# Attention of a two-layer trunk on one core: the order of its transposes, value products and scores on TensorE, and the layout of 768 keys

## The chip, the cores and the metric

The kernel runs on 1 core of one Trainium2 chip. The metric is the device time of one execution in microseconds; shown is the median of several executions. Where a profile is read, it is the profile of one execution.

## The reference, cut to what matters

A latent stream x of 512 tokens (a grid 64 wide) and 256 context tokens y pass two layers of width 1024. In each layer one input projection of 2976 columns feeds four mixers with 4 heads each; their 4 x 256 outputs go through one output projection into a gated residual, then a SwiGLU block of hidden width 2816 follows. Three of the mixers are softmax attention, and they are what the change touches:

```python
def softmax_attend(q, k, v, scale, sink=None):
    s = einsum('bhqd,bhkd->bhqk', q, k) * scale        # sink: one more logit
    return einsum('bhqk,bhkd->bhqd', softmax(s), v)
# mla: latent queries read 512 latent + 256 context keys, q and k of 64 + 32 rotary columns
# na:  neighbourhood attention, 8 x 16 of the grid, with a bias, and the 256 context keys, one softmax
# swa: windowed attention, 128 keys to either side, the context keys and a sink logit
# context queries read the 256 context keys only, in all three (layer 0; in layer 1 only x goes on)
```

The fourth mixer is a bidirectional chunkwise retention. Everything is float32.

## The kernel before, in words

Tokens are handled in tiles of 128: tiles 0 to 3 are latent, 4 and 5 context (in layer 1 only 0 to 3 as queries). A dense product is made of three matmuls (`mm3`, L467 to L469): weights and activations are split into a high part and a remainder.

**Weights.** A block of weights, 512 KB as a rule, is loaded into a tile `raw` (four buffers in the kernel before: the line `CHANGED`), copied by ScalarE into `wh` (L449), and the remainder `wl` is made by VectorE or, one time in three, by GpSimd (`sub_lo`, L213). After these two the raw buffer is free. `load_nat` does this for a projection: 8 row blocks of 128, two to a block, so 4 blocks for 512 columns; its loads are on SyncE's queue (L459). The feed-forward weights are loaded from ScalarE's queue (L1454, L1494).

**Stages of a layer.** `na_proj` (two projections), `na_attn`, `swa_proj`, `swa_attn`, `ret_proj` (two projections), `mla_proj` with the retention chunks `ret_chunk`, then a loop over the tiles `mo`: MLA attention of a tile (`mla_attn`), a number of half output projections that don't need it (`rest`, numbers `FILL`), `merge_mla`, which splits the result for the output projection, and `finish`, the other half, with the norm for the feed-forward block. Then the feed-forward block in 11 groups of 256 hidden columns.

**Attention of a tile.** `q_stack` loads q, transposes it (L669), and splits it into `qa` by ScalarE (L673) and `qb` by VectorE (L674); MLA adds a rotary part (L989 to L993). For each head: scores into PSUM tiles `s` (`scores`, L633; L935 to L937 in na, L1142 to L1147 in swa), the minimum of the negated scores (MLA: L1007, two pieces of 384 keys, and L1009), the exponential on ScalarE with its sum (L1012, L1155, L1157, L946), and the division `norm_p` (L614, L620). `attend_T` then transposes the probabilities P (L586) into PSUM tiles `t` and copies them to `PT`, the first four blocks by ScalarE (L589), the rest by VectorE (L591). `attend_pv` makes the value products of two heads (a pair) into a tile `o` (L599).

**What sets the order.** The program is traced in the order of the code, and a planner then orders each engine's instructions: it runs the program on a model of its own, takes what is ready, and so moves instructions of later stages ahead of ones that wait. Each kind of tile has a fixed number of buffers (`s` 4 of the PSUM banks, `t` 2, `o` 2, `P` 6, `PT` 4, `qT` 3, `wh` 5, `wl` 7, `raw` 4); the planner places them in memory and makes an instruction wait for a buffer. On the chip an engine runs its queue in that order.

Of the kernel before, what the change touches and what calls it, by code (L numbers as in the profile page):

```python
# [16 lines left out]
P = 128  # L17
# [60 lines left out]
CHANGED = {'pad': {'raw': 1024}, 'bufs': {'raw': 4}}  # L78
# [9 lines left out]
def build(tc, I, out, opts=None):  # L88
# [85 lines left out]
    TR = (opts or {}).get("tr", ("ldq", "ldq", "xn"))  # L174
    PRI = {}
# [459 lines left out]
    def soft_y(q_of, k_of, v_of, negsink=None, sk=None):  # L635

        pv = PS("o")
        sums = S("s2", 8).rearrange("p (h a) -> p h a", h=H)
        m = S("m4", 4)
        for hp in range(2):  # L640
            A = PS("s")
            for e in range(2):
                h = 2 * hp + e
                scores(A[:, 256 * e:256 * e + 256], q_of(h), k_of(h))
# [4 lines left out]
            PTs = []  # L649
            for e in range(2):  # L650
# [7 lines left out]
                PTs.append(attend_T(Pm, 2))  # L658
            attend_pv(pv, hp, PTs, [v_of(2 * hp), v_of(2 * hp + 1)])
        return pv  # L660
# [150 lines left out]
    for l in range(LAYERS):  # L811
# [28 lines left out]
        def na_proj():  # L840
# [76 lines left out]
            def na_attn():  # L917
                st = T("st", [P, 2, NT])
                for t in () if last else ytiles:
                    o = soft_y(q_stack(qn_d[rows(t), :], -0.125), lambda h: [kTn[h][:, NX:NT]] * 2,  # L920
                               lambda h: [Vyn[:, i, h * 64:(h + 1) * 64] for i in range(2)])
                    put(o, st[:, :, rows(t)])
                for cb in range(4):
# [3 lines left out]
                    qs_ = q_stack(qn_d[rows(cb), :], -0.125)  # L927
                    pv = PS("o")
                    sums = S("s4", 4)
                    for h in range(H):  # L930
# [3 lines left out]
                        q2 = qs_(h)  # L934
# [11 lines left out]
                        act.activation(Pm, A, AF.Exp, bias=m[:, 0:1], scale=-1.0, accum_out=sums[:, h:h + 1])  # L946
                        dsl = slice(h * 64, (h + 1) * 64)
                        if h % 2 == 0:
                            PTs, vs = [], []
                        vs.append([Vw[(2 * cb + b) // 3][:, (2 * cb + b) % 3, dsl] for b in range(2)]  # L950
                                  + [Vyn[:, b, dsl] for b in range(2)])
                        norm_p(Pm, sums[:, h:h + 1])
                        PTs.append(attend_T(Pm, 4))
                        if h % 2:
                            attend_pv(pv, h // 2, PTs, vs)
                    put(pv, st[:, :, 0:NX].rearrange("p a (r c) -> p a r c", c=64)[:, :, :, 16 * cb:16 * cb + 16])
# [4 lines left out]
        def mla_proj(R):  # L961
# [19 lines left out]
            def mla_attn(t):  # L981
# [12 lines left out]
                qof = lambda h: q2(h) + [qr[:, h, :]]  # L994
                kof = lambda h, a, b: [kTm[h][:, a:b], kTm[h][:, a:b], kTr[:, a:b]]
                vof = lambda h, js: [Vm[j // 3][:, j % 3, h * 64:(h + 1) * 64] for j in js]
                if t >= 4:
                    return soft_y(qof, lambda h: kof(h, NX, NT), lambda h: vof(h, (4, 5)))
                pv = PS("o")
                s2 = S("s2", 8).rearrange("p (h a) -> p h a", h=H)  # L1000
                for h in range(H):
                    m2 = S("m2", 2)
                    A = []
                    for i in range(2):
                        A.append(PS("s")[:, 0:384])
                        scores(A[i], qof(h), kof(h, 384 * i, 384 * i + 384))
                        dve.tensor_reduce(m2[:, i:i + 1], A[i], axis=AX.X, op=ALU.min)  # L1007
                    m = S("m1", 1)
                    dve.tensor_tensor(m, m2[:, 0:1], m2[:, 1:2], op=ALU.min)  # L1009
                    Pm = T("P", [P, 768])  # L1010
                    for i in range(2):
                        act.activation(Pm[:, 384 * i:384 * i + 384], A[i], AF.Exp, bias=m[:, 0:1], scale=-1.0,  # L1012
                                       accum_out=s2[:, h, i:i + 1])
                    if h % 2 == 0:
                        PTs = []
                    norm_p(Pm, s2[:, h])
                    PTs.append(attend_T(Pm, 6))
                    if h % 2:
                        attend_pv(pv, h // 2, PTs, [vof(h - 1, range(6)), vof(h, range(6))])
                return pv  # L1020
# [26 lines left out]
            for t, ps in nat_block(w_in, 0, 416, hT, order, (lambda t: (0, 416) if (t < 4 or not last) else (160, 416))):  # L1047
# [52 lines left out]
                yield mla_attn  # L1100

        def swa_proj():
# [18 lines left out]
            def swa_attn():  # L1121
                st = T("st", [P, 2, NT])
                for t in (0, 1, 2, 3) + (() if last else ytiles):
                    qof = q_stack(q_d[rows(t), 384:640], -0.125)
                    vof = lambda h, js: [Vs[:, j, 64 * (h // 2):64 * (h // 2) + 64] for j in js]
                    if t >= 4:
                        o = soft_y(qof, lambda h: [kTs[h // 2][:, NX:NT]] * 2, lambda h: vof(h, (4, 5)),
                                   negsink=sinkn[:, l], sk=sink[:, l])
                    else:
                        lo_b = max(t - 1, 0)  # L1130
                        hi_b = min(t + 1, 3)
                        blks = list(range(lo_b, hi_b + 1))
                        nl = len(blks)
                        pv = PS("o")
# [403 lines left out]
```

## Time and profile before

| | us |
|---|---|
| median of 3 runs | 1907.11 |
| lowest and highest | 1906.93, 1912.47 |
| the profiled execution | 1910.68 |
| its span (first to last instruction) | 1908.8 |

The profiled execution is longer than its span by what lies around it. In all rows times are microseconds unless marked ns; PE is TensorE's matmul, PEld its weight load, DVE VectorE, ACT ScalarE, POOL GpSimd, SP SyncE, and a q behind a name is that engine's DMA queue. L and a number is a line of the kernel. Busy time counts pipelined matmuls with modelled ends, so a busy PE is not PE at its peak. `[0.96 <-DMA raw]` at the end of a row is the idle time of that engine just before, and what ended it.

### The profile page before, as it was taken

The numbers are of one execution on the slowest core, as the hardware profiler recorded it, in microseconds if no ns is written. First come the engines' busy times: TensorE is split into PE (matmuls) and PEld (weight loads), VectorE is DVE, ScalarE is ACT, GpSimd is POOL, SyncE is SP. The second block draws the span as 40 slices with busy tenths as digits, with TensorE's granted clock in tenths as the row PEclk, the third lists the DMA queues.
The fourth block names the chain that finished last, engine by engine and source line by source line (L and its number), as shares of the span: only waits on it lengthen the run. The fifth ranks groups of instructions, "written<-read, shape, count | busy, mean of one in ns | idle before, by whom it ended". The sixth has DMA issues, their size and how long they took to land. (4 is left out here: it accounts for less than half of the span.)

```text
span 1908.8 us, 28192 instructions
## 1 busy us (share of the span) xinstructions
PE 1811.7 (95%) x10447; PEld 1494.0 (78%) x10447; DVE 1187.5 (62%) x2676; ACT 672.9 (35%) x1517; POOL 605.2 (32%) x560
## 2 busy tenths in 40 slices
PE   6899999889999999999999999899889999999997
PEld 3677777778889887888888878788777888888885
DVE  5696886877898757564434293465588863434335
ACT  3325643254542221221122233564255532222223
POOL 0211113323115443444344111211333144645542
PEclk9999999899999999999999999999999999999999
DMA  7675436445124346342222222422443033232321
GB/s 226 210 206 162 131 98 187 127 151 117 50 95 127 122 155 199 105 134 63 74 67 67 57 84 91 120 75 81 143 142 100 15 115 101 84 107 89 102 86 44
DMA packets 193555, 215.22 MB, mean 113 GB/s; under 512 B 66660, under 2 KB 141578, under 8 KB 193418
## 3 DMA queue, kind: packets, MB, share of 16 engines
q10 hardware_dynamic: 75840, 111.17, 18.8%
q1 hardware_dynamic: 117578, 102.25, 18.1%
q8 instruction: 82, 1.34, 0.3%
q14 instruction: 55, 0.45, 0.1%
HBM read 192.76 MB, written 20.63 MB: 112 GB/s over the span
## 5 line engine op out<-in xcount | busy, mean ns | idle before, releaser
L469 PE MATMUL pg<-wh,b 128*128 128x512 f32 (+2 forms) x1128 | 439.9, 394 | 7.2 <-POOL b L213 6.2
L467 PE MATMUL pg<-wh,b 128*128 128x512 f32 (+2 forms) x1128 | 443.1, 393 | 1.8 <-ACT b L515 0.9
L468 PE MATMUL pg<-wl,b 128*128 128x512 f32 (+2 forms) x1128 | 441.5, 391 | 2.2 <-DVE rs_yn L288 1.8
L467 PE MATMUL ps<-b,wh 128*128 128x512 f32 (+1 forms) x1120 | 388.2, 347 | 0.0
L469 PE MATMUL ps<-b,wl 128*128 128x512 f32 (+1 forms) x1120 | 386.7, 345 | 0.8 <-DVE wl L213 0.8
L468 PE MATMUL ps<-b,wh 128*128 128x512 f32 (+1 forms) x1120 | 386.9, 345 | 0.5 <-POOL b L213 0.5
L213 DVE TENSOR_TENSOR wl<-raw,wh 128x1024 fp32r<-128x1024 f32 (+1 forms) x131 | 207.4, 1592 | 174.9 <-ACT wh L449 145.3
L449 ACT ACTIVATE wh<-raw 128x1024 fp32r<-128x1024 f32 (+1 forms) x196 | 203.8, 1049 | 271.1 <-PE pg L469 172.3
L213 POOL TENSOR_TENSOR wl<-raw,wh 128x1024 fp32r<-128x1024 f32 (+1 forms) x65 | 160.0, 2462 | 336.7 <-ACT wh L449 286.8
L1362 POOL TENSOR_TENSOR b<-b,nat 128x512 f32<-128x512 f32 (+1 forms) x204 | 217.8, 1087 | 124.0 <-DVE nat L1360 95.0
L469 PEld LDWEIGHTS pg<-wh,b 128*128 128x128 f32 x1128 | 214.9, 191 | 49.6 <-POOL b L213 9.6
L467 PEld LDWEIGHTS pg<-wh,b 128*128 128x128 f32 x1128 | 215.5, 191 | 40.9 <-ACT b L1476 1.9
L468 PEld LDWEIGHTS pg<-wl,b 128*128 128x128 f32 x1128 | 215.2, 191 | 39.7 <-DVE rs_yn L288 2.3
L467 PEld LDWEIGHTS ps<-b,wh 128*128 128x128 f32 x1120 | 213.5, 191 | 27.4 <-issue 2.4
L469 PEld LDWEIGHTS ps<-b,wl 128*128 128x128 f32 x1120 | 213.4, 191 | 26.0 <-DVE wl L213 1.0
L468 PEld LDWEIGHTS ps<-b,wh 128*128 128x128 f32 x1120 | 213.6, 191 | 25.5 <-POOL b L213 0.7
L1360 DVE TENSOR_TENSOR nat<-pg,gate 128x512 f32<-128x512 f32 x240 | 161.9, 688 | 102.0 <-PE pg L469 97.8
L1473 ACT ACTIVATE P<-ps 128x512 f32<-128x512 f32 (+1 forms) x70 | 35.4, 505 | 224.3 <-PE ps L469 128.0
L1475 DVE TENSOR_TENSOR P<-ps,P 128x512 f32<-128x512 f32 (+1 forms) x70 | 40.1, 575 | 118.9 <-PE ps L469 118.8
L1476 ACT ACTIVATE b<-P 128x512 fp32r<-128x512 f32 (+1 forms) x70 | 37.6, 538 | 195.3 <-DVE P L1475 176.0
L397 DVE SCALAR_TENSOR_TENSOR PT<-qT,consts,PT 128x512 f32<-128x512 f32 x112 | 94.0, 857 | 14.6 <-DMA qT<-in_ada_w_dram 13.3
L213 POOL TENSOR_TENSOR b<-P,b 128x512 fp32r<-128x512 f32 (+1 forms) x24 | 27.8, 1158 | 231.9 <-ACT b L1476 231.9
(322 smaller groups left out, 2441.7 us busy)
## 6 DMA issues: line engine op xcount, KB each, us to landing
raw<-in_ffn_w_dram ACTq DMA_DIRECT2D x132, 512.0 KB
qT<-in_ada_w_dram ACTq DMA_DIRECT2D x96, 256.0 KB
raw<-in_w_in_dram SPq DMA_DIRECT2D x40, 512.0 KB
a<-in_ada_w_dram SPq DMA_DIRECT2D x32, 256.0 KB
a<-in_ada_w_dram ACTq DMA_DIRECT2D x32, 256.0 KB
xn<-in_ada_w_dram ACTq DMA_DIRECT2D x32, 256.0 KB
raw<-in_w_out_dram SPq DMA_DIRECT2D x16, 512.0 KB
ldq<-q_d SPq DMA_DIRECT2D x40, 128.0 KB
```

The lines of the kernel that those rows point to most:

```text
L213: eng.tensor_tensor(out, full, hi.bitcast(F32), op=ALU.subtract)
L397: dve.scalar_tensor_tensor(acc[s], w, sS[:, k, s:s + 1], acc[s], op0=ALU.mult, op1=ALU.add)
L449: act.activation(hi, raw_ap, AF.Copy)
L467: pe.matmul(ps, a[0], b[0], start=first, stop=False)
L468: pe.matmul(ps, a[0], b[1], start=False, stop=False)
L469: pe.matmul(ps, a[1], b[0], start=False, stop=last)
L1360: dve.tensor_tensor(tm, ps, gates[(0 if t < 4 else 2) + b], op=ALU.mult)
L1362: eng.tensor_tensor(ap, ap, tm[:, a:c], op=ALU.add)
L1473: act.activation(s1[j][:, sl], ps, AF.Silu)
L1475: dve.tensor_tensor(s1[j][:, sl], ps, s1[j][:, sl], op=ALU.mult)
L1476: act.activation(gh[j][:, sl], s1[j][:, sl], AF.Copy)
```

## The change

The attention functions no longer run a head after the other. Each returns or pushes jobs, one for a pair of heads (`hp`), with a function `s` that traces the scores and the softmax and gives the two P tiles, and a function `fin` for what is to be done with the result. `Flow` takes the jobs with a depth of 2: when a third pair is pushed, a turn is traced first, which has the transposes of the oldest pair's second head, the value products of the pair before it, and the transposes of its first head; then come the scores of the pushed pair. `part` uses `tc.issue_after`: each TensorE instruction traced inside is queued behind the last TensorE instruction of the part before (an edge for the order of issue alone, no wait for its end). Instructions of other stages are not bound by it. The q of a tile is now made inside the scores of its first pair.

In MLA the 768 keys of a pair's two heads lie in three banks: the first head in one whole bank and half of the second, the second head in the other half and the third. One minimum covers each bank. In `swa` the tiles whose window has only two blocks (t = 0 and 3) put window and context keys in one bank, with one minimum and one exponential. `raw` has two buffers. `merge_mla` is now called when the value products of a tile's second pair are traced.

`na_attn` is changed as the others: its loop body becomes a function `soft(cb, hp, cell)` with the same instructions for two heads, pushed into a flow of its own, and so is `swa_attn`; both drain their flow at the end. The rest of the diff, cut to its core:

```diff
-CHANGED = {'pad': {'raw': 1024}, 'bufs': {'raw': 4}}
+CHANGED = {'pad': {'raw': 1024}, 'bufs': {'raw': 2}, 'depth': (2, 2, 2)}
...
+    DEPTH = (opts or {}).get("depth", (1, 1, 1))
...
+    def last_pe():
+        return next(i for i in reversed(nc.cur_bb.bb.instructions) if i.engine == pe.engine)
+    class Flow:
+        def __init__(self, depth):
+            self.depth, self.todo, self.prev, self.last = depth, [], None, None
+        def part(self, f, *a):
+            if self.last is None:
+                f(*a)
+            else:
+                with tc.issue_after(self.last):
+                    f(*a)
+            self.last = last_pe()
+        def trans(self, j, e):
+            j["pt"][e] = attend_T(j["p"][e], j["n"])
+        def values(self, j):
+            if j["hp"] == 0:
+                j["cell"]["pv"] = PS("o")
+            attend_pv(j["cell"]["pv"], j["hp"], j["pt"], j["vs"])
+            if j["hp"] == 1:
+                j["fin"](j["cell"]["pv"])
+        def turn(self):
+            j = self.todo.pop(0)
+            self.part(self.trans, j, 1)
+            if self.prev is not None:
+                self.part(self.values, self.prev)
+            self.part(self.trans, j, 0)
+            self.prev = j
+        def push(self, j):
+            if len(self.todo) == self.depth:
+                self.turn()
+            j["pt"] = [None, None]
+            self.part(lambda: j.update(p=j["s"]()))
+            self.todo.append(j)
+        def drain(self):
+            while self.todo:
+                self.turn()
+            self.part(self.values, self.prev)
...
+    def soft_y(q_of, k_of, v_of, fin, negsink=None, sk=None):
+        cell = {}
+        def soft(hp):
+            if hp == 0:
+                cell["q"] = q_of()
+                cell["sums"] = S("s2", 8).rearrange("p (h a) -> p h a", h=H)
+                cell["m"] = S("m4", 4)
+            sums, m = cell["sums"], cell["m"]
...
+                        cell["q"] = mla_q(t)
+                        cell["sums"] = S("s2", 8).rearrange("p (h a) -> p h a", h=H)
+                    A = [PS("s") for _ in range(3)]
+                    cuts = (((A[0], 0, 512), (A[1][:, 0:256], 512, 768)), ((A[1][:, 256:512], 0, 256), (A[2], 256, 768)))
+                    m4 = S("m4", 4)
+                    for e in range(2):
+                        for ps, a, b in cuts[e]:
+                            scores(ps, cell["q"](2 * hp + e), kof(2 * hp + e, a, b))
+                        if e == 0:
+                            dve.tensor_reduce(m4[:, 0:1], A[0], axis=AX.X, op=ALU.min)
+                    dve.tensor_reduce(m4[:, 1:3], A[1].rearrange("p (a b) -> p a b", a=2), axis=AX.X, op=ALU.min)
+                    dve.tensor_reduce(m4[:, 3:4], A[2], axis=AX.X, op=ALU.min)
+                    m = S("m2", 2)
+                    dve.tensor_reduce(m, m4.rearrange("p (a b) -> p a b", a=2), axis=AX.X, op=ALU.min)
+                    res = []
+                    for e in range(2):
+                        Pm = T("P", [P, 768])
+                        for i, (ps, a, b) in enumerate(cuts[e]):
+                            act.activation(Pm[:, a:b], ps, AF.Exp, bias=m[:, e:e + 1], scale=-1.0,
+                                           accum_out=cell["sums"][:, 2 * hp + e, i:i + 1])
+                        norm_p(Pm, cell["sums"][:, 2 * hp + e])
+                        res.append(Pm)
+                    return res
+
+                return [dict(s=lambda hp=hp: soft(hp), n=6, hp=hp, cell=cell, fin=fin,
+                             vs=[vof(2 * hp, range(6)), vof(2 * hp + 1, range(6))]) for hp in range(2)]
...
+                        if nl == 2:
+                            AB = PS("s")
+                            A, B = AB[:, 0:256], AB[:, 256:512]
+                        else:
                             A = PS("s")[:, 0:nl * P]
                             B = PS("s")[:, 0:256]
...
+                        if nl == 2:
+                            dve.tensor_reduce(m3[:, 0:1], AB, axis=AX.X, op=ALU.min)
+                            dve.tensor_tensor(mh, m3[:, 0:1], sinkn[:, l, h:h + 1], op=ALU.min)
+                            act.activation(Pm, AB, AF.Exp, bias=mh, scale=-1.0, accum_out=s3[:, h, 0:1])
+                            act.activation(s3[:, h, 1:2], mh, AF.Exp, bias=sink[:, l, h:h + 1])
+                            norm_p(Pm, s3[:, h, 0:2])
...
-        for i, mla_attn in enumerate(mla):
+        for i, mla_pairs in enumerate(mla):
             if ret_todo:
                 ret_chunk(ret_todo.pop(0))
             rest(FR[l][1 + i])
+        flow = Flow(DEPTH[2])
         for i, t in enumerate(mo):
-            if t % 2 == 0 and MR == 0:
+            if t % 2 == 0:
                 merge_ret(t // 2)
-            o = mla_attn(t)
-            if MM:
-                merge_mla(t, o)
+            for j in mla_pairs(t, lambda pv, t=t: merge_mla(t, pv)):
+                flow.push(j)
+            if t == mo[-1]:
+                flow.drain()
             rest(FILL[l][i] if i < len(mo) - 1 else 12)
-            if not MM:
-                merge_mla(t, o)
-            if t % 2 == 0 and MR == 1:
-                merge_ret(t // 2)
             finish(FIN[l][i])
```

## Rows read from the trace of the kernel before

**Rows 1.** The page's busy times of the whole span: busy, share, instructions.

```profile
PE 1811.7 (95%) x10447; PEld 1494.0 (78%) x10447; DVE 1187.5 (62%) x2676; ACT 672.9 (35%) x1517; POOL 605.2 (32%) x560
```

**Rows 2.** Windows of attention: length, busy (instructions) of each engine, granted clock, DMA share, GB/s.

```profile
142.00:316.00 174.00, 165.77 (x1175) 129.42 (x1174) 137.07 (x368) 93.03 (x275) 23.00 (x21) 0.99 0.46 135
436.00:524.00 88.00, 87.95 (x611) 71.78 (x610) 67.01 (x174) 48.28 (x130) 23.40 (x25) 1.00 0.28 68
1213.00:1329.00 116.00, 114.46 (x886) 95.37 (x887) 74.25 (x229) 70.57 (x196) 15.69 (x11) 0.99 0.24 70
1432.00:1517.00 85.00, 82.57 (x585) 68.32 (x583) 71.70 (x196) 44.04 (x118) 15.46 (x15) 1.00 0.23 62
```

**Rows 3.** Waits of PE, 142 to 316 us: who, for whom, total, times, longest.

```profile
PE ps L633 <- DVE qT L674: 4.4, 3, 2.1
PE pt L586 <- DVE P L620: 1.8, 3, 1.0
...
PE pt L586 <- DVE sm L611: 0.4, 1, 0.4
PE pt L586 <- DVE rc L614: 0.2, 1, 0.2
```

**Rows 4.** Waits of PE, 1213 to 1329 us.

```profile
PE pt L669 <- DMA ldq<-qn_d: 3.0, 1, 3.0
...
PE pt L586 <- DVE P L620: 0.2, 1, 0.2
```

**Rows 5.** Waits of PE, 1432 to 1517 us.

```profile
PE po L599 <- DVE PT L591: 1.4, 1, 1.4
PE pt L586 <- DVE P L620: 0.8, 1, 0.8
```

**Rows 6.** Groups by line, the q split: shape, count, busy, mean ns, idle before.

```profile
L674 DVE SCALAR_TENSOR_TENSOR qT<-pt,qT 128x512 fp32r<-128x512 f32 x30 | 20.7, 689 | 26.7 <-ACT qT L673 26.2
...
L673 ACT ACTIVATE qT<-pt 128x512 fp32r<-128x512 f32 x30 | 17.9, 597 | 5.5 <-PE pt L669 5.0
```

**Rows 7.** Groups by line and form: minima on DVE, exponentials on ACT.

```profile
L1007 DVE TENSOR_REDUCE m<-ps 128x1 f32<-128x384 f32 x64 | 33.7, 548 | 5.1 <-PE ps L633 5.0
L1151 DVE TENSOR_REDUCE m<-ps 128x1 f32<-128x256 f32 x32 | 13.2, 414 | 0.1
L646 DVE TENSOR_REDUCE m<-ps 128x2 f32<-128x512 f32 x12 | 7.7, 685 | 1.6 <-PE ps L633 1.5
L1009 DVE TENSOR_TENSOR m<-m 128x1 f32<-128x1 f32 x32 | 4.9, 153 | 0.3
...
L946 ACT ACTIVATE P<-ps,m 128x512 f32<-128x512 f32 x32 | 21.8, 686 | 18.7 <-PE ps L633 10.8 <-DVE m1b L941 2.7 <-DMA xn<-in_ada_w_dram 2.3
L1157 ACT ACTIVATE P<-ps,m 128x256 f32<-128x256 f32 x32 | 15.1, 471 | 0.0
```

**Rows 8.** A window after the first layer's MLA.

```profile
530.00:560.00 30.00, 28.18 (x164) 24.54 (x165) 29.56 (x68) 15.05 (x28) 8.00 (x5) 1.00 0.17 54
```

**Rows 9.** Timeline, raw blocks from 119 to 139 us: start, duration, what, idle before.

```profile
119.48 1.47 SPq L459 DMA_DIRECT2D raw<-in_w_in_dram  x2
...
123.56 0.39 SPq L459 DMA_DIRECT2D raw<-in_w_in_dram  x1
...
124.53 1.06 ACT L449 ACTIVATE wh<-raw 128x1024 fp32r<-128x1024 f32 x1 [0.96 <-DMA raw<-in_w_in_dram]
...
125.67 2.60 POOL L213 TENSOR_TENSOR wl<-raw,wh 128x1024 fp32r<-128x1024 f32 x1 [33.73 <-ACT wh L449]
...
130.60 2.00 ACT L449 ACTIVATE wh<-raw 128x1024 fp32r<-128x1024 f32 x2
```

**Rows 10.** Waits over the whole span.

```profile
ACT wh L449 <- PE pg L469: 172.3, 32, 15.1
```

**Rows 11.** Timeline of PE at 342 us, and the window around it.

```profile
342.37 0.69 PE L1282 MATMUL ps<-ldr,P 128*128 128x64 f32 x2 [6.71 <-DVE P L1270]
330.00:366.00 36.00, 28.11 (x173) 23.65 (x172) 28.75 (x83) 10.46 (x22) 12.36 (x13) 0.76 0.41 126
```

More of the change, by code (lines that the diff above doesn't have):

```diff
@@ L643, in soft_y @@
                 h = 2 * hp + e
-                scores(A[:, 256 * e:256 * e + 256], q_of(h), k_of(h))
+                scores(A[:, 256 * e:256 * e + 256], cell["q"](h), k_of(h))
             mh = m[:, 2 * hp:2 * hp + 2]
@@ L918, in na_attn, with soft @@
                 st = T("st", [P, 2, NT])
+                flow = Flow(DEPTH[0])
                 for t in () if last else ytiles:
[L920 to L923, printed above, removed]
+                    for j in soft_y(lambda t=t: q_stack(qn_d[rows(t), :], -0.125), lambda h: [kTn[h][:, NX:NT]] * 2,
+                                    lambda h: [Vyn[:, i, h * 64:(h + 1) * 64] for i in range(2)],
+                                    lambda pv, t=t: put(pv, st[:, :, rows(t)])):
+                        flow.push(j)
+                def soft(cb, hp, cell):
                     et = (0, 1, 1, 2)[cb]
@@ L926, in na_attn @@
                     w0 = W0[cb]
[L927 to L930, printed above, removed]
+                    if hp == 0:
+                        cell["q"] = q_stack(qn_d[rows(cb), :], -0.125)
+                        cell["sums"] = S("s4", 4)
+                    res = []
+                    for h in (2 * hp, 2 * hp + 1):
                         A = PS("s")
@@ L997, in mla_attn @@
                 if t >= 4:
[L998 to L1019, printed above, removed]
@@ L1122, in swa_attn @@
                 st = T("st", [P, 2, NT])
[L1123 to L1134, printed above, removed]
-                        s3 = S("s3", 12).rearrange("p (h a) -> p h a", h=H)
-                        m = S("m4", 4)
-                        for h in range(H):
+                flow = Flow(DEPTH[1])
@@ new lines, in soft @@
+                        if t > 0:
+                            pe.matmul(A[:, 0:P], identb, swmask[:, 0, :], start=False, stop=(t == 3))
+                        if t < 3:
+                            pe.matmul(A[:, (nl - 1) * P:nl * P], identb, swmask[:, 1, :], start=False, stop=True)
+                        scores(B, q2, [kTs[h // 2][:, NX:NT]] * 2)
+                        m3 = S("m3", 2)
+                        mh = m[:, h:h + 1]
+                        Pm = T("P", [P, nl * P + 256])
+                        if nl == 2:
[4 more added lines that the diff above has]
+                            norm_p(Pm, s3[:, h, 0:2])
+                        else:
@@ L1166, in swa_attn @@
-                        o = pv
-                    put(o, st[:, :, rows(t)])
+                        res.append(Pm)
+                    return res
+                for t in (0, 1, 2, 3) + (() if last else ytiles):
+                    fin_ = lambda pv, t=t: put(pv, st[:, :, rows(t)])
+                    if t >= 4:
+                        js = soft_y(lambda t=t: q_stack(q_d[rows(t), 384:640], -0.125), lambda h: [kTs[h // 2][:, NX:NT]] * 2,
+                                    lambda h: vof(h, (4, 5)), fin_, negsink=sinkn[:, l], sk=sink[:, l])
+                    else:
+                        blks = list(range(max(t - 1, 0), min(t + 1, 3) + 1))
+                        cell = {}
+                        js = [dict(s=lambda t=t, hp=hp, blks=blks, cell=cell: soft(t, hp, blks, cell), n=len(blks) + 2, hp=hp,
+                                   cell=cell, fin=fin_, vs=[vof(2 * hp, blks + [4, 5]), vof(2 * hp + 1, blks + [4, 5])])
+                              for hp in range(2)]
+                    for j in js:
+                        flow.push(j)
```

96 lines of the change are left out of this document (50 added, 46 removed).

## Prediction

> **What bounds the kernel now.** I began with the busy shares of the whole span: TensorE's matmul rows fill 95% of it [rows 1], so all its idle time is 97.1 us (1908.8 less 1811.7), over every stage. Then I cut out the stretches in which the attention's own transposes, scores and value products run, because only there does the change put another order: 142 to 316 and 436 to 524 us in the first layer, 1213 to 1329 and 1432 to 1517 us in the second [rows 2]. There the reader is to subtract TensorE's busy time from the length: 8.2, 0.05, 1.5 and 2.4 us idle, 12.2 us in 463. The granted clock is 0.99 to 1.00, the 2.4 GHz level, so nothing is to be won from the clock there. Attention does not leave TensorE empty, because the planner puts projection matmuls between its instructions; next in line is VectorE, 79% busy in the first stretch and 84% in the last.
>
> Last I asked what ended these idle times [rows 3 to 5]. Three kinds come out. Transposes that waited for a normalised P or its sums, and value products that waited for a copied PT: 1.8 + 0.4 + 0.2, then 0.2, then 1.4 + 0.8 = 4.8 us. Scores that waited for the split q: 4.4 us. A first q that came late by DMA: 3.0 us. So the kernel is bound by the amount of TensorE work, and the waits that a better order inside attention can remove are a quarter of a per cent.
>
> **The change part by part.** My sum is made against the profiled execution: 1910.7 us, a span of 1908.8 and 1.9 around it. It lies 3.6 us above the median of the runs, 1907.1, so I take 3.6 off at the end.
>
> *Order of the groups.* No matmul, transpose or value product is added or removed: an MLA pair has 12 score matmuls before (2 heads x 2 pieces x 3 terms) and after (2 x 2 x 3), over the same 768 keys. What changes is that the transposes of pair i come after the scores of pair i+1 have been queued, and the value products are those of pair i-1. Between a softmax and its transposes there is now a full turn, and between transposes and value products another one. The 4.8 us of waits for P and PT should go; I take all of it, -4.8. What is late next is the q of the next tile. Ends: 0, if the projection matmuls only move elsewhere, and -12.2, all the idle time of [rows 2].
>
> *The q stack.* It is now traced inside the scores' part, so its transposes are queued behind those of pair i. After them stand a ScalarE copy of 0.60 us and a VectorE operation of 0.69 us [rows 6], twice as much for MLA, whose rotary part has its own transposes and split, before the first score can run; behind that score on TensorE's queue stand the transposes and value products of the next turn, and ScalarE's softmax waits for them. There are 30 such stacks. Before, 3 waits of 4.4 us in all show in the first stretch; the others were covered by projection matmuls, which may still be put in between, since the new edges bind only the attention's own instructions. I take the 4.4 us as unchanged, 0. Ends: -4.4, and +19.4 if half of the 30 lie bare for 0.60 + 0.69 us.
>
> *Three banks for 768 keys.* A pair of MLA had four minima over 384 keys and two small ones, 4 x 0.548 + 2 x 0.153 = 2.50 us of VectorE; now three over 512 and one small one, 3 x 0.685 + 0.153 = 2.21 us [rows 7]. 0.29 us saved in each of 16 pairs (32 small minima stand in the row, one for each head): 4.7 us. In the window attention the first and last tile of a layer (16 heads) get one minimum over 512 keys for two over 256, 0.69 for 2 x 0.414 us: 2.3 us over all, the one-column operations left aside. ScalarE replaces two exponentials of 256 keys, 0.94 us, by one of 512, 0.69 us: 4.1 us over all [rows 7]. All of this lies beside TensorE work, so by itself I cost it at nothing. It counts only where VectorE is full: from 530 to 560 us, just after the first layer's MLA, VectorE is busy 29.56 of 30 us and TensorE idles 1.8 us [rows 8]. The eight pairs of that layer give VectorE 2.3 us back, so that idle time may go: -1.5. Ends: 0 and -1.8. On the other side a pair holds three of the four score banks at once; before, a head held two. The next pair's third bank is free only after the third exponential of this one, which the order forgives as long as a turn is longer than the three (0.69 + 0.47 + 0.47 us).
>
> *Two raw buffers in place of four.* This is the part that can cost. A weight block is loaded by SyncE, copied by ScalarE, and its remainder made by VectorE or GpSimd; only then is the buffer free. At 119 us four blocks are loaded nearly together [rows 9]: the first is issued at 119.48, begins to be copied at 124.53, and its remainder ends at 128.27. With two buffers the third load, issued at 123.56 before, can't go out before 128.3, so it lands at about 133.3 in place of 130.6 at the latest. One round of a buffer is about 8.8 us by these rows, and two buffers then give a block every 4.4 us. But copies mostly wait for something else: over the whole span ScalarE's copies stood 172.3 us behind TensorE, which had to be done with an older block first [rows 10]. Blocks are loaded long before their copies can begin, so I take 0. Ends: 0 and +21: six block changes (three changes of projection without attention between them, in two layers) of 3.5 us, the time by which the fourth block of a projection would be late if it is wanted 5.5 us after the first. It can't win anything by itself, unless the freed space lets other tiles be placed earlier; that I can't price from rows, so I allow it the idle time of one stage change.
>
> *What moves with it.* The planner orders all queues anew. One accident shows what that is worth: at 335 us TensorE waited 6.71 us for a masked P of the retention mixer, and the granted clock of 330 to 366 us is 0.76, partly at the 1.2 GHz level [rows 11]. VectorE's queue had other work ahead. Such a gap can go or come, 7 us and the slow clock behind it; I take 0 and keep -12 and +12 as an estimate (6.71 us, and about 5 us of the 8.6 lost where 36 us run at 0.76).
>
> Sum: -4.8 + 0 - 1.5 + 0 + 0 = -6.3; 1910.7 - 6.3 = 1904.4, less 3.6 is 1900.8. I forecast **1901 us**, 0.3% faster.
>
> The weight-load rows read this differently. They are busy 74.4, 81.6, 82.2 and 80.4% of the four stretches [rows 2]; measured by the third, the first lacks 9.5% or 16.5 us, the second 0.6 and the last 1.9 us, 19 us in place of 12.2. The Trainium skill ("Perfetto Trace Analysis", Identifying the Most-Contended Engine) says that busy time of pipelined matmuls is no measure of the distance to the peak and that busy time of weight loads is a better one. By that rule there is more to win, and the whole 19 us would make it 1888; the trace bears it out in the first stretch alone, where both measures show most room.
>
> **The rivals.**
> *Hidden anyway (same), 0.22.* The planner already interleaves: TensorE idles 0.05 us in the first MLA stretch [rows 2]. Then filling 4.8 us there only shortens the filler that would be wanted later, and the projections end when they did. For it: that row. Against it: the last stretch still idles. Time: 1906, between 1902 and 1911.
> *Weights come late (slower), 0.20.* Place: the changes of projection; mechanism: the third and fourth block of a projection are loaded only after the first two are split. Price 3.5 us each, six of them, less the 6.3: about 1922 at full price, 1914 at half. It decides once two of the six or more lie bare. For it: the just-in-time loads at 119 us [rows 9]. Against it: the 172.3 us [rows 10].
> *The q stack lies bare (slower), 0.08.* 15 x 1.29 us less 6.3: 1920. For it: the 4.4 us [rows 3]; against it: the filler that covered the other 27.
> *More room (faster), 0.10.* By the weight-load shares 1888; the same time if the gap at 335 us goes and the forecast comes in as well.
>
> **How the numbers follow.** The forecast has 0.40; its own range is 1894 to 1907. From no change, 0.3% (5.7 us) is about what a measurement of this kernel can tell. Faster: 0.28 of the forecast, 0.04 of the hidden case and the 0.10 of more room, 0.42. Same: 0.11 of the forecast, 0.18 of the hidden case, 0.01 of the late weights, 0.30. Slower: 0.19 of the late weights, 0.08 of the bare q and 0.01 of the forecast, 0.28. The range 1886 to 1922 leaves one in ten on either side: it reaches the full price of late weights, and the room by the weight loads nearly.
>
> **What would show it.** Right: in the attention stretches no transposes wait for P (L620) and no value products for PT; one minimum over 512 keys with a mean near 0.69 us; VectorE's busy time lower by about 7 us. Late weights: ScalarE's copies of raw blocks waiting for loads, and TensorE for the remainder of a block, near a change of projection. A bare q: scores waiting for the split q more than 3 times. The forecast is wrong if TensorE's idle time in the four stretches falls by less than 3 us, or if the time moves while it doesn't; then the plan elsewhere, or the buffers, made it.

## The result, and the profile after

The changed kernel takes 1927.7 us (median of four runs, 1924.0 to 1930.4); the kernel before took 1907.7 us on the same chip. The ratio is 1.0098, 95% interval 1.0071 to 1.0126: 1% slower where 0.3% faster was forecast, and above the upper end of the range, 1922 us. The profiled execution took 1925.2 us, its span is 1923.4 us, 14.6 longer than before.

First the page's busy times, which answer to [rows 1].

```profile
PE 1815.1 (94%) x10447; PEld 1491.1 (78%) x10447; DVE 1189.5 (62%) x2628; ACT 667.6 (35%) x1485; POOL 603.8 (31%) x560
```

Span less busy time leaves TensorE idle for 108.3 us against 97.1: 11.2 of the 14.6 us are idle time, and 3.4 are matmuls that lasted longer. To see where the idle time lies I cut the four attention stretches again, at the times by which TensorE had done the same work as at the edges of [rows 2].

```profile
143.00:323.00 180.00, 167.46 (x1182) 131.50 (x1181) 133.53 (x359) 91.67 (x262) 21.08 (x19) 0.97 0.45 133
442.00:534.00 92.00, 89.30 (x646) 72.39 (x645) 72.88 (x165) 47.64 (x129) 21.85 (x21) 1.00 0.26 66
1222.00:1340.00 118.00, 114.45 (x885) 94.08 (x883) 73.79 (x219) 67.27 (x180) 15.61 (x11) 1.00 0.29 86
1444.00:1531.00 87.00, 84.05 (x587) 68.53 (x586) 69.55 (x179) 44.16 (x124) 17.18 (x18) 0.98 0.32 84
```

Length less busy time: 12.5, 2.7, 3.6 and 3.0 us, 21.8 in all, where [rows 2] had 12.2. So 9.6 of the 11.2 us of new idle time lie in the very stretches in which some should have gone. The waits of TensorE in the four windows (one after another; who, for whom, total, times, longest) answer to [rows 3 to 5].

```profile
PE pt L587 <- ACT P L706: 4.4, 1, 4.4
PE pu L405 <- DVE ldr L398: 3.4, 1, 3.4
...
PE pt L587 <- DVE P L621: 1.6, 2, 1.3
PE ps L634 <- DVE qT L729: 1.5, 1, 1.5
...
PE pt L587 <- DVE P L621: 1.4, 2, 0.8
PE ps L634 <- DVE qT L1057: 0.7, 1, 0.7
...
PE pt L587 <- DVE P L621: 1.9, 2, 1.0
...
PE pt L587 <- ACT P L1088: 2.5, 1, 2.5
```

Transposes waited 11.8 us for a P (4.4 + 1.6 + 1.4 + 1.9 + 2.5); before, all waits for P, its sums and PT were 4.8. A full turn lies between a softmax and its transposes, and still they wait. Such a wait can have two reasons: the P is late, or TensorE has no projection matmuls left to put before it, and those need split weights. Behind the longest one, 4.4 us, the P was late. ScalarE stood for 7.35 us at an instruction that, by the profile, waited for the store of an earlier `nat` tile to land, and the exponentials stood behind it in ScalarE's queue:

```profile
159.25 0.28 ACT L737 ACTIVATE nat<-pg 128x128 fp32r<-128x128 f32 x1 [7.35 <-DMA qn_d<-nat]
...
162.56 0.66 PE L587 MATMUL pt<-consts,P 128*128 128x128 f32 x2 [4.39 <-ACT P L706]
```

For the weights I looked at the raw blocks, as in [rows 9]: the timeline of SyncE's loads, ScalarE's copies, the remainders and TensorE (start, duration, what, count, idle before).

```profile
118.16 0.91 SPq L460 DMA_DIRECT2D raw<-in_w_in_dram  x2
...
121.94 1.06 ACT L450 ACTIVATE wh<-raw 128x1024 fp32r<-128x1024 f32 x1
...
125.65 0.40 SPq L460 DMA_DIRECT2D raw<-in_w_in_dram  x1
...
129.99 0.39 SPq L460 DMA_DIRECT2D raw<-in_w_in_dram  x1
...
133.86 1.06 ACT L450 ACTIVATE wh<-raw 128x1024 fp32r<-128x1024 f32 x1 [2.20 <-DMA raw<-in_w_in_dram]
...
135.05 3.21 POOL L214 TENSOR_TENSOR wl<-raw,wh 128x1024 fp32r<-128x1024 f32 x1 [9.43 <-ACT wh L450]
...
138.32 0.50 PE L469 MATMUL pg<-wl,b 128*128 128x512 f32 x1 [2.84 <-POOL wl L214]
```

The third load goes out 7.5 us after the first two, when a buffer is free; the fourth another 4.3 us later. The fourth copy finds ScalarE waiting for it, and its remainder finds TensorE waiting, 2.84 us. From 128 to 166 us TensorE does 34.39 us of work before and 28.61 after, at a granted clock of 0.96 and 0.93. Of the 9.4 us that it idles there after (3.6 before), 2.84 are this wait for a remainder and 4.39 the late P above, so only a part of the difference is late weights (windows of the kernel before, then after):

```profile
128.00:166.00 38.00, 34.39 (x196) 25.89 (x195) 25.33 (x54) 17.99 (x57) 6.45 (x6) 0.96 0.64 178
```
```profile
128.00:166.00 38.00, 28.61 (x156) 21.04 (x155) 21.29 (x47) 14.42 (x42) 3.56 (x3) 0.93 0.61 171
```

Whether copies wait for their loads is told by lines of ScalarE's waits over the whole span, beside [rows 10]; before there is one,

```profile
ACT wh L449 <- DMA raw<-in_w_in_dram: 9.2, 4, 6.4
```

and after

```profile
ACT wh L450 <- PE pg L470: 206.0, 33, 14.7
...
ACT wh L450 <- DMA raw<-in_w_in_dram: 34.4, 13, 8.2
...
ACT wh L450 <- DMA raw<-in_ffn_w_dram: 17.4, 9, 5.1
...
ACT wh L450 <- DMA raw<-in_w_out_dram: 3.0, 1, 3.0
```

54.8 us in 23 waits, against 9.2 in 4. The line on which the forecast relied, copies waiting for TensorE, is longer too (206.0 against 172.3). Both can be true at once.

The stage of [rows 11] did not get worse: TensorE's longest wait near it is 3.36 us, and the window that answers has less idle time and the better clock (0.91, before 0.76). The window that answers to [rows 8] has VectorE still full and TensorE 2.1 us idle, as before:

```profile
345.36 1.12 PE L1320 MATMUL pu<-rt,o 128*64 128x128 f32 x8 [3.36 <-DVE rt L1316]
```
```profile
333.00:369.00 36.00, 29.14 (x188) 24.52 (x189) 31.21 (x81) 11.59 (x24) 15.85 (x23) 0.91 0.40 126
541.00:571.00 30.00, 27.93 (x169) 24.55 (x168) 30.00 (x78) 12.72 (x27) 5.00 (x3) 1.00 0.17 55
```

Of the groups in [rows 6, 7], the minima over 512 keys and the q split have the durations expected (columns as there):

```profile
L1079 DVE TENSOR_REDUCE m<-ps 128x1 f32<-128x512 f32 x16 | 11.0, 689 | 4.3 <-PE ps L634 4.0
...
L729 DVE SCALAR_TENSOR_TENSOR qT<-pt,qT 128x512 fp32r<-128x512 f32 x30 | 20.6, 685 | 15.2 <-ACT qT L728 15.2
```

### The profile page after: what moved, and what is told of

It is laid out like the page before. It is cut to its first block, busy times and chain, and to the rows that moved or that the text cites. A ratio compares the mean times of both kernels' runs of the same rounds, so it can differ in the third digit from the quotient of the medians.

```text
span 1923.4 us, 28159 instructions
## 1 busy us (share of the span) xinstructions
PE 1815.1 (94%) x10447; PEld 1491.1 (78%) x10447; DVE 1189.5 (62%) x2628; ACT 667.6 (35%) x1485; POOL 603.8 (31%) x560
## 2 busy tenths in 40 slices
DMA packets 193555, 215.22 MB, mean 112 GB/s; under 512 B 66660, under 2 KB 141578, under 8 KB 193418
## 3 DMA queue, kind: packets, MB, share of 16 engines
q10 hardware_dynamic: 75840, 111.17, 18.7%
## 4 chain that ended last, share of the span: by engine, by line
PE 57%; DVE 11%; DMA 3%; issue 2%; ACT 2%; POOL 2%; ACTq 0%; SPq 0%; DVEq 0%; POOLq 0%
PE ps L468 9%; PE ps L469 9%; PE ps L470 9%; PE pg L470 7%; PE pg L468 7%; PE pg L469 7%; PE ps L634 2%; PE pt L587 2%; PE po L600 2%; DVE wl L214 2%; ACT wh L450 1%; DVE nat L1454 1%; POOL wl L214 1%; DVE PT L398 1%; DVE ldq L515 1%
## 5 line engine op out<-in xcount | busy, mean ns | idle before, releaser
L450 ACT ACTIVATE wh<-raw 128x1024 fp32r<-128x1024 f32 (+1 forms) x196 | 204.0, 1050 | 338.7 <-PE pg L470 206.0
```

Of the source, the lines that this page charges most:

```text
L450: act.activation(hi, raw_ap, AF.Copy)
```

## The experiments

Every run stood beside the kernel before on its own chip, whose median was 1906.6 to 1908.8 us; ratios are to that, with 95% intervals. "Serial" is the changed kernel with each pair's scores, transposes and value products traced behind one another and no ordered group. The last column is what ScalarE's copies waited for loads of raw, over the span of the profiled execution. The other runs are given in the text. The changed kernel with turns in all three attentions and four whole buffers was not run; e3 and e8 come nearest.

| run | base | raw buffers | us | ratio | loads waited for |
|---|---|---|---|---|---|
| before | | 4 whole | 1907.7 | 1 | 9.2 us, 4 |
| after | turns | 2 whole | 1927.7 | 1.0098 (1.0071 to 1.0126) | 54.8 us, 23 |
| e1 | before | 2 whole | 1926.6 | 1.0098 (1.0083 to 1.0112) | 23.8 us, 18 |
| e5 | before | 3 whole | 1919.1 | 1.0063 (1.0047 to 1.0079) | 17.0 us, 9 |
| e2 | serial | 4 whole | 1915.8 | 1.0048 (1.0036 to 1.0060) | 8.8 us, 3 |
| e4 | serial | 2 whole | 1928.9 | 1.0111 (1.0095 to 1.0128) | 26.5 us, 19 |
| e3 | turns in window and MLA attention, neighbourhood serial | 4 whole | 1910.6 | 1.0020 (1.0009 to 1.0031) | 8.0 us, 2 |
| e8 | as e3, neighbourhood as before | 4 whole | 1911.8 | 1.0020 (1.0009 to 1.0031) | 8.3 us, 2 |
| e12 | as e3, neighbourhood as before | 2 whole | 1921.6 | 1.0060 (1.0039 to 1.0082) | 43.6 us, 22 |
| e13 | before | 4 half | 1914.5 | 1.0028 (1.0017 to 1.0040) | 16.1 us, 14 |
| e14 | before | 8 half | 1903.8 | 0.9977 (0.9964 to 0.9990) | 6.8 us, 5 |
| e17 | turns | 4 half | 1913.1 | 1.0019 (1.0007 to 1.0030) | 18.7 us, 12 |
| e15 | turns | 6 half | 1897.4 | 0.9939 (0.9915 to 0.9963) | 7.4 us, 7 |
| e18 | serial | 6 half | 1903.1 | 0.9970 (0.9959 to 0.9982) | 6.1 us, 4 |

**The buffers alone, and the ordered groups alone.** e1 is the kernel before with one number changed:

```diff
-CHANGED = {'pad': {'raw': 1024}, 'bufs': {'raw': 4}}
+CHANGED = {'pad': {'raw': 1024}, 'bufs': {'raw': 2}}
```

> The kernel before with two raw buffers in place of four, nothing else. Theory B (the buffers cost it: blocks are loaded late, and other work on the load queue stands behind loads that wait for a buffer): 1920 to 1930 us, +0.7 to +1.2%, as in the changed kernel. Theory O (the ordered groups cost it, the buffers are covered by the copies that wait for TensorE anyway): 1905 to 1911 us, no change. Theory P (no part has a price of its own, every new plan lands within some 10 us): anywhere from 1900 to 1918 us.

e2 to e4 are the changed kernel, its groups and its buffers set separately (a depth of 0 is serial; the order is neighbourhood, sliding window, MLA):

```diff
-CHANGED = {'pad': {'raw': 1024}, 'bufs': {'raw': 2}, 'depth': (2, 2, 2)}
+CHANGED = {'pad': {'raw': 1024}, 'bufs': {'raw': 4}, 'depth': (0, 0, 0)}  # e2; e3: (0, 2, 2); e4: raw 2
```

> The changed kernel without turns and without the edges: each pair is traced as scores, softmax, transposes of both heads, value products, then the next pair; four raw buffers. What is left of the change is the pairwise trace, the three banks for 768 keys and the one bank for two blocks of window attention. Theory B: 1903 to 1909 us, a little better for the VectorE time saved. Theory O: the same, 1903 to 1909 us. If it is slower than 1912 us, the layout of the scores has a price (three of four score banks held at once).

> The changed kernel with turns and edges in window attention and MLA alone, neighbourhood attention traced pair after pair; four raw buffers. Theory B: 1900 to 1908 us, the turns are harmless or help where buffers are not short. Theory O: 1914 to 1922 us, two thirds of the ordered groups and so two thirds of the loss. Theory P: 1900 to 1920 us.

> As the second of these runs (pair after pair, no turns, no edges), but with two raw buffers. Theory B: 1920 to 1930 us, 15 to 20 us over its twin with four. Theory O: 1904 to 1910 us, as its twin. Theory P: within 10 us of its twin, either way.

e1 loses as much as the changed kernel without a line of the new attention: ratio 1.0098. The same wait stands in its timeline, two loads together, the rest one by one, and TensorE at the end:

```profile
116.27 0.93 SPq L459 DMA_DIRECT2D raw<-in_w_in_dram  x2
...
123.68 0.40 SPq L459 DMA_DIRECT2D raw<-in_w_in_dram  x1
...
131.99 1.06 ACT L449 ACTIVATE wh<-raw 128x1024 fp32r<-128x1024 f32 x1 [2.30 <-DMA raw<-in_w_in_dram]
...
133.19 3.11 POOL L213 TENSOR_TENSOR wl<-raw,wh 128x1024 fp32r<-128x1024 f32 x1 [9.53 <-ACT wh L449]
...
136.34 0.50 PE L468 MATMUL pg<-wl,b 128*128 128x512 f32 x1 [2.74 <-POOL wl L213]
```

e2 lies 7 us above what Theories B and O both expected: the new layout and the tracing by pairs, without groups, cost 0.48%. e3 shows that groups in two attentions win 0.28 of that back, so Theory O, that the groups cost, falls (its 1910.6 us lie between the ranges of B and O). e4 against e2: two buffers cost 0.63% here.

**How much, and is it the plan?** The planner orders every queue anew at each edit, so a loss could be chance of the plan (Theory P). e5 sets three buffers, e6 two with the weights issued by GpSimd, e7 the score layout alone:

```diff
+CHANGED = {'pad': {'raw': 1024}, 'bufs': {'raw': 3}}                          # e5
+CHANGED = {'pad': {'raw': 1024}, 'bufs': {'raw': 2}, 'q': {'wn': 'pool'}}     # e6
+A = [PS("s") for _ in range(3)]   # e7: MLA pair in three banks; first and last window tile in one
```

> The kernel before with three raw weight buffers in place of four; nothing else differs. It gives the dose between 1906.9 us (four) and 1926.6 us (two). Theory L (late blocks: each buffer that is missing delays the four loads of a projection block a little): about half of the 19.7 us, 1913 to 1920 us. Theory H (head of the line: it is the loads that queue on SP behind a waiting weight load which cost it, and three buffers still leave one always waiting): 1920 to 1928 us. Theory T (a threshold: only two are too few, since the split of a third overlaps the loads of the first two): 1904 to 1910 us.

> The kernel before with two raw buffers, and the loads of the projection weights issued from GpSimd in place of SyncE, so that no other load stands behind one that waits for a buffer. Theory H (what queues on SP behind the weights costs it): most of the 19.7 us comes back, 1906 to 1913 us. Theory L (the blocks themselves are late): 1920 to 1930 us as with two buffers on SP; the activation copies of raw would still wait for loads and TensorE for wl and wh. If GpSimd now waits at the loads and delays its own remainders, it is slower than both, over 1930 us.

> The kernel before, four buffers, with the score layout of the changed kernel alone: 768 keys of a pair in three banks in MLA, and one bank for the tiles of two key blocks in sliding-window attention; neighbourhood attention stays head by head, no ordered groups. If the 9 us by which the ungrouped changed kernel with four buffers lay above before (1915.8 against 1906.9 us) come from this layout: 1912 to 1918 us. If they come from tracing both heads of a pair together in neighbourhood attention and the text tiles, or from the plan that this gives: 1903 to 1909 us.

Three buffers lie between, 1.0063, as Theory L has it, so it is not a threshold; the interval, up to 1.0079, reaches into the range of Theory H. e6 took 1933.5 us (1.0140, 1.0119 to 1.0161); there GpSimd itself waited, for room in raw, so whether loads queued behind the weights on SyncE add to the loss stays open:

```profile
POOL raw L459 <- DVE wl L213: 101.6, 21, 26.0
```

e7 took 1919.1 us (1.0060, 1.0041 to 1.0079): the layout, with the two heads of an MLA pair traced together as it requires, costs as much as e2 lost, with neighbourhood attention still head by head. e8 and e12 put neighbourhood attention back as it was, under the turns of the other two; e9 to e11 are edits that should do nothing or help:

```diff
+def na_attn(): ...                                                    # e8, e12: as before, depth (2, 2, 2), raw 4 and 2
+CHANGED = {'pad': {'raw': 1024}, 'bufs': {'raw': 4, 'nat': 3}}        # e9;  e10: 'o': 2
-for cb in range(4):
+for cb in (1, 0, 3, 2):                                               # e11
```

> The changed kernel with four buffers and with neighbourhood attention as before (head by head), turns in sliding-window and MLA attention. Its twin with neighbourhood attention traced pair by pair took 1910.6 us. If the pairwise tracing of neighbourhood attention is what costs: 1900 to 1906 us, the fastest of all. If it costs nothing: 1908 to 1913 us.

> Turns in sliding-window and MLA attention, neighbourhood attention as before, with two raw buffers; its twin with four took 1911.8 us. If the price of the buffers is their own, whatever the plan (Theory B): 13 to 20 us more, 1925 to 1932 us, as in the two pairs so far (1906.9 to 1926.6, 1915.8 to 1928.9). If it is mostly the plan of before that four buffers happen to suit (Theory P): 1911 to 1919 us.

> The kernel before with one more buffer for the natural-order tiles (nat: three in place of two), all else as before, raw at four. A further buffer can only take a wait away, but TensorE's instructions come out in another order over long stretches. Theory P (any other plan than that of before costs some microseconds, which then is part of every run so far): 1911 to 1919 us. Without P: 1899 to 1908 us.

> The kernel before with one more buffer for the output tiles of retention (o: two in place of one), raw at four: the same question with a smaller replanning. Theory P: 1909 to 1917 us. Without P: 1900 to 1908 us, with the wait of the store of o (26.9 us of SyncE's in eight) gone.

> The kernel before with the four column blocks of neighbourhood attention in the order 1, 0, 3, 2: the same instructions on each engine, the same waits, only their order a little different within one stage of each layer. Theory P with its smallest dose: 1908 to 1913 us. Without P, and as what a neutral edit of one stage is worth: 1904 to 1909 us.

e9 took 1906.8 us (0.9990, 0.9977 to 1.0003), e10 1912.5 (1.0020, 1.0007 to 1.0033), e11 1906.3 (0.9988, 0.9978 to 0.9998). These three replannings moved the time by -0.12 to +0.20%; e10 lies in the range of Theory P, e9 and e11 do not. e8 against e3 shows no price or gain of the tracing of neighbourhood attention (both 1.0020). Two buffers for four cost 0.98, 0.63 and 0.40% in three pairs (e1, e4 against e2, e12 against e8). e12 lies between the ranges of Theories B and P: the size depends on the plan; the sign was the same in all three pairs.

**Which step of a buffer's cycle, and a way out.** e13 and e14 halve the raw buffer: each half is loaded, copied, split and released by itself.

```diff
-raw = T("raw", [P, 2, n])
-Q["wn"].dma_start(raw, v[:, kh:kh + 2, c0:c0 + n])
-hi, lo = split_unit(raw, [2, n])
+for i in range(2):      # hi, lo as before; the same for the other weights
+    raw = T("raw", [P, n])
+    Q["wn"].dma_start(raw, v[:, kh + i, c0:c0 + n])
+    act.activation(hi[:, i], raw, AF.Copy)
+    sub_lo(lo[:, i], raw, hi[:, i])
```

e15 and e17 are the changed kernel so (`'pad': {'raw': 512}, 'bufs': {'raw': 6}` and 4), e18 is e15 with depth (0, 0, 0). e16 keeps two whole buffers and fetches half the columns:

```diff
-Q["wn"].dma_start(raw, v[:, kh:kh + 2, c0:c0 + n])
+Q["wn"].dma_start(raw[:, :, 0:n // 2], v[:, kh:kh + 2, c0:c0 + n // 2])  # copy and remainder read it twice
```

> The kernel before with raw buffers of half the size: four of 2 KB per partition, the bytes of two, each filled by a 256 KB load and released after its own copy and its own remainder (so twice the copies, remainders and loads, at half the size). Theory G (grain: what costs in the two-buffer runs is that a load of 512 KB can only start when a copy and a remainder over all of its buffer are done): half-size buffers turn over in half the time, 1910 to 1918 us. Theory S (the bytes in flight count, a load must be issued a fixed time ahead): 1922 to 1930 us, like two. The doubled instructions cost something in either case.

> Control: raw buffers of half the size, eight of them, the bytes of four. It prices the doubling of copies, remainders and loads by itself: 1905 to 1912 us if these lie beside TensorE's work, 1915 to 1925 us if VectorE and ScalarE have no room for them.

> The kernel before with two raw buffers, where each load of a projection block's weights fetches the first half of the columns only, which the copy and the remainder then read twice (half of those weights are left out; instructions of the engines are the same in number and size). Theory L with the transfer as its cost: the landing comes sooner, and half or more of the 19.7 us come back, 1908 to 1917 us. If the time is in the turnover of the buffers (waiting for the copy and the remainder, not for the bytes): 1920 to 1928 us.

> The changed kernel, turns in all three attentions, with six raw buffers of half the size: 12 KB per partition in place of 8. Theory B (its loss is the buffers' price, 13 to 20 us, plus the layout's and the plan's, 5 to 12, less the turns' gain): half to two thirds of the buffers' price come back, 1913 to 1920 us against 1927.7 us. If grain gives nothing: 1925 to 1931 us.

> The changed kernel with four raw buffers of half the size: exactly the bytes of its two whole ones, in a finer grain. Theory G (the turnover of whole buffers is what the changed kernel paid for): as in the kernel before (1926.6 to 1914.5 us with the same bytes) some 12 to 20 us come back, 1906 to 1915 us. Theory S (bytes in flight; six halves helped by their four further KB alone): 1920 to 1930 us.

> The twin of the changed kernel with six half-size buffers (1897.4 us), without turns and without an ordered group: each pair's scores, transposes and value products traced behind one another, all else the same. If the ordered groups are worth the 5 us that two of the attentions gave with four whole buffers, or more: 1902 to 1912 us. If they are worth nothing and the 1897.4 us come from the buffers and the layout: 1894 to 1900 us.

e13 holds the bytes of e1 and is 12 us faster: the grain counts. e17 shows it on the changed kernel itself, 1927.7 to 1913.1 us with the same bytes and the same groups. e16, 1913.7 us (1.0030, 1.0014 to 1.0046), gets as much back with half the bytes of the weights that `load_nat` brings. Whether that is the shorter transfer of a block, or that 16 MB less are moved beside all other loads (198.84 MB, 215.22 before), is not told apart. It is not shorter waits of the copies: they stood 38.0 us in 20 waits for loads, more than the 23.8 us in 18 of e1.

```profile
ACT wh L449 <- DMA raw<-in_w_in_dram: 27.7, 15, 7.4
...
ACT wh L449 <- DMA raw<-in_ffn_w_dram: 10.3, 5, 5.3
```

So the last column of the table tells that loads come late, but it does not measure the loss; e12, with 43.6 us, also loses less than e1. e14's doubled instructions cost nothing that shows beside what the finer grain may give. e15 is the fastest of all, 16 us below the lower end of what was expected of it, and no run explains the whole of that. In its timeline the loads of the same stage go out four and three at a time:

```profile
119.06 1.78 SPq L473 DMA_DIRECT2D raw<-in_w_in_dram  x4
...
120.27 0.62 ACT L464 ACTIVATE wh<-raw 128x512 fp32r<-128x512 f32 x1
...
123.86 1.30 SPq L473 DMA_DIRECT2D raw<-in_w_in_dram  x3
```

e18, without groups, is 5.7 us slower than e15 (0.9970 against 0.9939; the two intervals just overlap). The four stretches, cut as above, first e15 and then e18:

```profile
138.00:310.00 172.00, 165.26 (x1188) 129.84 (x1187) 137.43 (x371) 94.07 (x273) 22.44 (x23) 0.99 0.49 150
436.00:526.00 90.00, 88.38 (x642) 71.80 (x641) 73.36 (x166) 47.84 (x133) 21.97 (x23) 1.00 0.24 60
1208.00:1324.00 116.00, 113.59 (x883) 93.89 (x882) 77.46 (x225) 67.53 (x188) 19.48 (x16) 1.00 0.28 83
1427.00:1511.00 84.00, 82.15 (x578) 67.58 (x578) 68.44 (x169) 42.92 (x121) 16.46 (x17) 1.00 0.24 62
```
```profile
139.00:312.00 173.00, 164.43 (x1177) 129.06 (x1176) 134.41 (x365) 92.81 (x267) 23.89 (x22) 0.99 0.46 136
434.00:528.00 94.00, 89.36 (x607) 70.18 (x607) 72.72 (x168) 48.22 (x133) 27.02 (x27) 1.00 0.26 63
1210.00:1327.00 117.00, 114.05 (x884) 94.58 (x884) 74.47 (x225) 69.63 (x189) 18.66 (x15) 0.99 0.25 75
1429.00:1515.00 86.00, 83.61 (x589) 67.33 (x588) 72.58 (x179) 43.36 (x121) 16.49 (x17) 1.00 0.24 63
```

TensorE idles 12.6 us with turns and 18.6 without, and this difference is just the one that the turns were made for: transposes and value products waited 3.6 us for P and PT with turns, 9.6 without. These are the lines that make the 3.6 us of e15, then the longest of e18:

```profile
PE pt L599 <- DVE P L633: 1.6, 3, 0.7
...
PE pt L599 <- ACT PT L602: 0.7, 1, 0.7
...
PE pt L599 <- DVE P L633: 1.3, 2, 0.9
```
```profile
PE po L612 <- ACT PT L602: 2.4, 1, 2.4
...
PE pt L599 <- DVE m L1103: 1.5, 1, 1.5
...
PE pt L599 <- DVE P L633: 1.6, 3, 1.2
```

(The two profiled spans are only 2 us apart, 1901.1 and 1903.1; the 5.7 us are of the medians.)

## Why the prediction was wrong

The forecast's own sign of being wrong came: TensorE's idle time in the four stretches did not fall by 3 us, it rose by 9.6. On one path the runs add up to the result: the layout, serial with four buffers, costs 0.48% (e2), two buffers 0.63% more (e4, 1.11%), and the groups take 0.13% back (after, 0.98%; this last step is inside the intervals). The parts are not independent: two buffers alone cost 0.98% (e1), and on top of them the serial layout adds only 0.13% (e4).

*Two raw buffers (taken at 0, ends 0 and +21)* is the step that failed. On the changed kernel itself a finer grain at the same bytes gives 15 us back (e17), and e1 shows 20 us on the kernel before; the value taken, 0, was wrong. The rival "weights come late" named the cause, and the third and fourth block do come as it says: issued one by one at 125.65 and 129.99 us, when a buffer is free. The error was in reading [rows 10]: the 172.3 us say that a copy whose data lie ready waits for its place in wh. They say so of a kernel with four buffers, where loads were issued early enough; they don't say how much earlier than needed. The rows that bear on two buffers were [rows 9], and there the slack was short. A sum of waits that a resource now hides is no measure of the slack once the resource is halved.

That the upper end, +21, came near the 20 us of e1 is luck, for it was worked out from six block changes at which TensorE waits 3.5 us. TensorE's own waits for split weights in the changed kernel are 5.0 us (4.0 for GpSimd's remainders, 1.0 for a copy), 1.1 before. (The rival's half price was also added up wrongly: 1907.1 + 10.5 - 6.3 is 1911, not 1914.) By which way late blocks cost the rest stays open. It is tempting to put it down to waits for P inside attention, where projection matmuls that should stand between are not ready. The pair e2 and e4 speaks against that as the main way: with four and with two buffers TensorE idles 16.6 and 16.1 us in the four stretches, cut as above, and waits 10.2 and 11.5 us for P and PT. And e14, faster than the kernel before, idles 19.0 us there.

A part of the price is matmuls that last longer. For the same 10447 matmuls TensorE is busy, in the profiled executions, 1819.5 us in e1 and 1811.7 before, 1818.0 in e4 and 1811.4 in e2, 1819.0 in e12 and 1809.8 in e8. The granted clock, as a mean of all executions, was 0.9826 against 0.9851, 0.9814 against 0.9838, and 0.9835 against 0.9865; over 1812 us of work that makes 4 to 6 us in each pair, an estimate from these figures. In e15 it was 0.9893 against 0.9847 for the kernel before on its chip, by the same estimate some 8 of the 10.6 us that it gains. No run shows what lowered or raised the clock.

*Order of the groups (-4.8)* had the mechanism right where buffers were not short, and the size in part by luck. In e15 against e18 the waits for P and PT fall by 6.0 us, and the medians lie 5.7 apart; with four whole buffers, in two attentions of three, the gain is 5.2 (e3 against e2). But the sum was to remove the 4.8 us of the kernel before, and these gains are against the new layout traced serially, which has twice those waits; against the kernel before, e15 has 1.2 us fewer. With two whole buffers the groups give 1.2 us, inside the intervals, and the waits stay: 11.8 us in the changed kernel, 11.5 in e4. With the same bytes in halves, e17, they are 5.6. That the turns lack the projection matmuls which late weights hold back is a reading that fits; the longest wait of the changed kernel had another reason, the store.

*The q stack (0)* held: scores waited 1.5 and 0.7 us for the split q in the four stretches, 4.4 before.

*Three banks (-1.5)* was wrong in sign with four whole buffers: e7 costs 0.60%, outside what the three small replannings moved (at most 0.20%). With half-size buffers the same layout and its serial trace cost nothing (e18 with six, 0.9970; e14 with eight, 0.9977). The rows of the minima in MLA and window attention did fall as summed, from 74.2 to 66.7 us, but VectorE's total did not fall by 7 us: it rose by 2.0 with 48 instructions fewer, so its other rows grew. Whether the three banks held at once, the tracing by pairs or the plan they led to is the cause was not settled.

*Replanning (0, 12 either way)* was allowed too much as far as three small edits show: they moved the time by -2 to +4 us. The gap of [rows 11] shrank, as it could.

*The weight-load measure* gave 1888 as the room. The fastest run, 1897.4, is 10.6 us below before on its chip; its four stretches lost no idle time against [rows 2] (12.6 against 12.2), so it gained elsewhere, and these rows neither bear the measure out nor refute it.

## What to carry to other kernels

When a change halves the buffers of a prefetch, cost it by the cycle of one buffer (wait for release, load, copy, remainder) against the time between uses, at the place where the loads go out latest, and not by how long the consumer waits for something else today. If the space is short, try the same bytes in smaller buffers, each released as soon as its own part is used, before giving up depth. Here an order that needs other work between its steps removed 6 us of waits where buffers were not short, and none where they were. And a sum of waits for loads tells that loads come late, not what that costs: e16 had more of them than e1 and was 13 us faster.

## What was not expected of the hardware

Halving the tile of a copy costs little more time in all: a copy of 1024 columns took 1.06 us and one of 512 columns 0.62 us on ScalarE. In e14 that raised ScalarE's busy time from 672.9 to 694.4 us and VectorE's from 1187.5 to 1220.6 us over the span, and the kernel was not slower (0.9977, 0.9964 to 0.9990); no run has the doubling without the finer grain.
